# Feed-forward down products by Strassen's seven block products, placed between up products

## The chip, the cores and the metric

One core of a Trainium2 chip runs the whole program. The metric is the device time of one execution in microseconds (us), the median of several runs.

## What is computed

Two post-norm residual layers on 256 tokens of width 2048, all in float32. Layer 0 mixes tokens with a bidirectional gated linear attention, layer 1 with a two-dimensional neighbourhood attention. After each comes a gated feed-forward part, which the change is about:

```
D_FF = 11 * D_MODEL // 4                 # 5632, or 44 blocks of 128

def _conv_ffn(x, w_up, conv_w, conv_b, w_down):
    h = x @ w_up                         # 256 x 11264
    hp = jnp.pad(h, ((0, 0), (1, 1), (0, 0)))
    h = hp[:, :-2] * conv_w[0] + hp[:, 1:-1] * conv_w[1] + hp[:, 2:] * conv_w[2] + conv_b
    a, b = jnp.split(h, 2, axis=-1)
    return (jax.nn.gelu(a, approximate=False) * b) @ w_down

x = _layer_norm(DEEPNORM_ALPHA * x + f, ln_ffn_g[i], ln_ffn_b[i])
```

## The kernel before, in words

**Precision.** Every large product is made of three: each operand is split into a high part, which is the value rounded to the matrix unit's float32r type, and a low part, the rest. High times high, high times low and low times high are summed. `emit_split` (L129) does the split: a cast on ScalarE (L130), then a subtraction on VectorE (L131).

**Weights.** All weight matrices are cut into units of 1 MB, 128 x 2048 elements, and `unit_plan` (L48) lists them in the order of their use. SyncE's queue loads them (`emit_load`, L121) into three buffers, `pump` (L133) splits them in two halves, up to four units ahead of their use (NS = 4), with a scheduling rank 20 instructions later than where the split is written. `take` and `finish` (L159, L166) hand a unit to its product and release it. The framework orders each engine's instructions by rank and by its own estimate of when each is ready, and makes the semaphores; on the chip each engine then runs its list in order.

**Up products.** `ws_one` (L203) makes 128 channels of an up product for all 256 tokens: for each of 16 blocks of the width, a 512-column matmul (high part of the weights against high and low parts of both token halves) and a 256-column one (low part of the weights against the high parts). All matmuls go through `mm` (L191), so they share L192. The two halves of the sum stand in different columns of a PSUM bank, and `join` (L498) adds them: a copy on ScalarE, a sum on VectorE. `conv` (L673) does the middle tap on GpSimd (L684), and the outer taps on VectorE (L685, L686). `evac` (L692) applies GELU to the first of two channel blocks (L697), multiplies by the second (L702) and splits the product into gT, the operand of the down product. The first two channel blocks of each half come out of one wide product that is transposed ("pairs", `pair` at L714), with the middle tap on ScalarE (L682).

**Down products.** The 44 channel blocks are taken in three parts of 16, 16 and 12 (`THIRDS`, L39). After the up products of a part, `residual_out` (L367) runs its down product over four blocks of 512 columns: `as_block` (L218) takes the units (512 rows by 512 columns of the matrix), and makes 24 matmuls of 512 columns with each: 4 row blocks, 2 token halves, 3 parts. The result is added to the residual x_sb from PSUM (L381 for the first part, with the residual's factor, L383 for the others). After the last part the LayerNorm follows (`ln_mid`, L289, or `ln_last`, L328). In `ln_mid`, `turn` transposes the normalised rows and writes the next operand, and `resid` (L314) scales the residual and adds the bias with an accumulating DMA from GpSimd's queue (L318).

**PSUM.** Of eight banks five serve the products (`ps_mm`, L109), three the transposes and the attention (`ps_tp`).

**Attention.** `score` (L755) and `pv` (L790) each have bursts of six 256-column matmuls, in sums of three or six in PSUM.

Of the kernel before, what the change touches and what calls it, by code (L numbers as in the profile page):

```python
# [10 lines left out]
F32 = mybir.dt.float32  # L11
# [6 lines left out]
P = 128  # L18
# [17 lines left out]

FF = 11 * D // 4
NCT = FF // P
THIRDS = ((0, 16), (16, 16), (32, 12))  # L39

NS = 4
NR = 3
TP = 3
SPLIT_AFTER = 20
LN_BEFORE = 30


def unit_plan():  # L48

    plan = []  # L50
    for h in range(HG):
        plan += [("ws", "gla_in", h * 2 + c) for c in range(2)]
        plan += [("ws", "gla_in", 8 + h * 2 + c) for c in range(2)]
        if h == 0:
            plan += [("lr",)]
        plan += [("as", "gla_in", 4 + h, u) for u in range(4)]
        plan += [("as", "gla_in", 8 + h, u) for u in range(4)]
    plan += [("as", "gla_out", nb, u) for nb in range(4) for u in range(4)]
    for layer in range(DEPTH):
        if layer == 1:  # L60
# [5 lines left out]
        for c0, n in THIRDS:  # L66
            if c0 == 0:
                plan += [("pairs", f"up{layer}", u) for u in range(4)]
            for c in range(c0 + (2 if c0 == 0 else 0), c0 + n):
                plan += [("ws", f"up{layer}", c), ("ws", f"up{layer}", NCT + c)]  # L70
            plan += [("as", f"down{layer}", nb, u)
                     for nb in range(4) for u in range(c0 // 4, (c0 + n) // 4)]
    return plan


# [1 line left out]
def kernel(  # L77
# [16 lines left out]
    nc = tc.nc  # L94
    plan = unit_plan()
    n_units = len(plan)
    slot, n = {}, 0
    for j, u in enumerate(plan):
        slot[j] = n
        n += u[0] != "lr"  # L100
# [11 lines left out]
    def ps_tp():  # L112
        return psum.tile([P, 512], F32, tag="tp", name="ps_tp", bufs=TP)
# [4 lines left out]
    def pieces(n):  # L118
        return [slice(c * 2048 // n, (c + 1) * 2048 // n) for c in range(n)]

    def emit_load(j):  # L121
        r = raw_p.tile([P, 2048], F32, tag="raw", name="raw")
        if plan[j][0] == "lr":
            nc.sync.dma_start(r[:, :512], w_lr)
        else:
            nc.sync.dma_start(r, w[slot[j]])
        raws[j] = r

    def emit_split(src, hi, lo):  # L129
# [3 lines left out]
    def pump():  # L133
        while st["split"] < min(n_units, st["done"] + NS):
            j = st["split"]
            while st["load"] < min(n_units, j + NR):
                emit_load(st["load"])
                st["load"] += 1
            r = raws.pop(j)
# [51 lines left out]
    def mm(o, l, r, start, stop):  # L191
        nc.tensor.matmul(o, l, r, start=start, stop=stop)  # L192


    def ws_part(xs, hi, lo, ps, kcs):
        hi3 = hi.rearrange("p (k m) -> p k m", m=P)
        lo3 = lo.rearrange("p (k m) -> p k m", m=P)
        ps4 = ps.rearrange("p (t h n) -> p t h n", t=2, h=2)
        for kc in kcs:
            mm(ps, hi3[:, kc], xs[:, kc].rearrange("p t h n -> p (t h n)"), kc == 0, False)  # L200
            mm(ps4[:, :, 0], lo3[:, kc], xs[:, kc, :, 0], False, kc == KC - 1)

    def ws_one(xs, evac):  # L203
        hi, lo = take()
# [84 lines left out]
    def ln_mid(pool, xs, t, stats, idx, gb):  # L289

        def head():
            mv, rstd = ln_head(pool, xs, t, stats)
            for b in range(4):
                blk = xs[:, t, b * 512:b * 512 + 512]
                nc.vector.tensor_scalar(blk, blk, mv[:, 0:1], rstd, ALU.subtract, ALU.mult)  # L295

        def turn(b):
# [62 lines left out]
        return g  # L360

    def load_gb(pool, idx):
        b = pool.tile([P, D], F32, tag="b", name="b")
        nc.gpsimd.dma_start(b, lnp[idx, 1:2, :].broadcast_to([P, D]))
        return load_g(scope["xp"], idx), b

# [298 lines left out]
    def ffn(layer):  # L665
# [4 lines left out]
        cb = pool.tile([P, 2 * NCT], F32, name="cb")  # L670
        nc.gpsimd.dma_start(cb, convb[:, layer])

        def conv(i, ch, ps, joined=False):  # L673
            if joined:
                hh = ps
            else:
                hh = pool.tile([P, T], F32, tag="h", name="h", bufs=3)
# [3 lines left out]
            if joined:  # L681
                nc.scalar.activation(c, hh, AF.Identity, bias=cb[:, ch:ch + 1], scale=w_[:, 1:2])  # L682
            else:
# [5 lines left out]
        for part, (c0, n) in enumerate(THIRDS):  # L689
            held = {}  # L690

            def evac(i, ps, joined=False):  # L692
                kc = i // 2
                if i % 2 == 0:
                    c = conv(0, c0 + kc, ps, joined)
                    ge = pool.tile([P, T], F32, tag="ge", name="ge", bufs=2)
                    nc.scalar.activation(ge, c, AF.Gelu)  # L697
                    held["a"] = ge
                else:
                    c = conv(1, NCT + c0 + kc, ps, joined)  # L700
                    gg = pool.tile([P, T], F32, tag="gg", name="gg", bufs=2)
                    nc.vector.tensor_tensor(gg, held["a"], c, ALU.mult)  # L702
                    emit_split(gg.rearrange("p (t n) -> p t n", t=2), gT[:, kc, :, 0], gT[:, kc, :, 1])

            start = 0
            if part == 0:

                ht = {}

                def h_out(t, ps):  # L710
                    ht[t] = pool.tile([P, 512], F32, tag="ht", name="ht", bufs=2)
                    nc.scalar.copy(ht[t], ps)

                def pair(i):  # L714
                    tp = ps_tp()
                    for j in range(2):
                        for t in range(2):
                            nc.tensor.transpose(tp[:, j * T + t * P:j * T + t * P + P],
                                                ht[t][:, (2 * j + i) * P:(2 * j + i) * P + P], ident)
                    for j in range(2):  # L720
                        evac(2 * i + j, tp[:, j * T:j * T + T], True)

                as_block(xT, 4, h_out, apart=True, settle=True)
                later(lambda: pair(0), 1)
                later(lambda: pair(1), 1)
                start = 4
            for i in range(start, 2 * n):
                ws_one(xT, lambda ps: evac(i, ps))
            if part == 0:
                scope["gb"] = load_gb(pool, idx) if idx == 2 * DEPTH - 1 else load_g(scope["xp"], idx)  # L730
            residual_out(gT, part == 0, part == len(THIRDS) - 1, n // 4, idx)


    def attention():
# [110 lines left out]
def lay_out(a):  # L845
# [7 lines left out]
    plan = [u for u in plan if u[0] != "lr"]  # L853
    w = np.empty((len(plan), P, 2048), np.float32)
    for dst, unit in zip(w, plan):
        m = mats[unit[1]]
        if unit[0] == "pairs":
            u = unit[2]
# [56 lines left out]
```

## Time and profile before

| | |
|---|---|
| median of 3 runs | 2282.26 us (2282.12 to 2282.65) |
| the profiled execution's own time | 2282.44 us |
| its span, from the first to the last instruction | 2280.6 us |
| mean granted clock of the matrix unit | 0.998 of full speed |
| busy share of the span: TensorE, VectorE, ScalarE, GpSimd | 99%, 66%, 46%, 14% |
| moved by DMA | 439.02 MB |

The profile is of one execution. PE is the matrix unit's matmuls, PEld its weight loads, which run beside the matmuls; DVE is VectorE, ACT ScalarE, POOL GpSimd, SP SyncE. The ends of matmuls are modelled, so their starts are what counts; some records of matmuls can be missing. An instruction is named by its line, its engine, and what it writes and reads.

### The profile page before, as it was taken

The numbers are of one execution on the slowest core, as the hardware profiler recorded it, in microseconds if no ns is written. First come the engines' busy times: TensorE is split into PE (matmuls) and PEld (weight loads), VectorE is DVE, ScalarE is ACT, GpSimd is POOL, SyncE is SP. The second block draws the span as 40 slices with busy tenths as digits, with TensorE's granted clock in tenths as the row PEclk, the third lists the DMA queues.
The fourth block names the chain that finished last, engine by engine and source line by source line (L and its number), as shares of the span: only waits on it lengthen the run. The fifth ranks groups of instructions, "written<-read, shape, count | busy, mean of one in ns | idle before, by whom it ended". The sixth has DMA issues, their size and how long they took to land. (4 is left out here: it accounts for less than half of the span.)

```text
span 2280.6 us, 29636 instructions
## 1 busy us (share of the span) xinstructions
PE 2262.1 (99%) x11740; PEld 1925.1 (84%) x11740; DVE 1506.3 (66%) x2096; ACT 1056.7 (46%) x1537; POOL 317.7 (14%) x272
## 2 busy tenths in 40 slices
PE   9999999999999999999999999999999999999997
PEld 7888888888888888888888888888888888888886
DVE  7656656866656665676686666667676567756775
ACT  6654544544434444344464555446444444434442
POOL 1101000222002220122010100001220022201211
PEclk9999999999999999999999999999999999999999
DMA  8544464745554445555585555547446555565452
GB/s 279 187 168 169 182 243 157 250 184 185 203 188 181 185 178 209 186 184 185 185 258 187 194 189 198 202 165 240 176 176 227 195 175 179 183 216 188 174 198 93
DMA packets 66602, 439.02 MB, mean 193 GB/s; under 512 B 7648, under 2 KB 9952, under 8 KB 15136
## 3 DMA queue, kind: packets, MB, share of 16 engines
q1 hardware_dynamic: 60336, 415.00, 50.1%
q0 software_dynamic: 5840, 21.61, 3.8%
q8 instruction: 92, 1.51, 0.3%
q10 hardware_dynamic: 288, 0.52, 0.1%
q14 instruction: 46, 0.38, 0.0%
HBM read 431.87 MB, written 2.10 MB: 190 GB/s over the span
## 5 line engine op out<-in xcount | busy, mean ns | idle before, releaser
L131 DVE TENSOR_TENSOR lo<-raw,hi 128x1024 fp32r<-128x1024 f32 (+1 forms) x791 | 943.2, 1210 | 486.6 <-ACT hi L130 485.6
L192 PE MATMUL ps_mm<-xT,hi 128*128 128x512 f32 x3472 | 1229.3, 399 | 2.4 <-ACT hi L130 1.8
L130 ACT CAST hi<-raw 128x1024 fp32r<-128x1024 f32 (+1 forms) x791 | 806.7, 1041 | 514.3 <-PE ps_mm L192 485.1
L192 PE MATMUL ps_mm<-xT,lo 128*128 128x256 f32 x3472 | 974.5, 281 | 0.2 <-DVE lo L131 0.2
L192 PEld LDWEIGHTS ps_mm<-xT,hi 128*128 128x128 f32 x3472 | 651.7, 188 | 162.6 <-ACT hi L130 2.6
L192 PEld LDWEIGHTS ps_mm<-xT,lo 128*128 128x128 f32 x3472 | 655.3, 189 | 1.5 <-DVE lo L131 0.8
L192 PE MATMUL ps_mm<-hi,gT 128*128 128x512 f32 x1920 | 594.6, 390 | 0.0
L192 PEld LDWEIGHTS ps_mm<-hi,gT 128*128 128x128 f32 x1920 | 360.2, 188 | 74.5
L684 POOL TENSOR_SCALAR c<-h,cw,cb 128x256 f32<-128x256 f32 x168 | 239.0, 1422 | 1070.2 <-DVE h L503 1070.2
L192 PE MATMUL ps_mm<-lo,gT 128*128 128x512 f32 x960 | 373.5, 389 | 0.0
L192 PE MATMUL ps_mm<-hi,xT 128*128 128x512 f32 x896 | 284.1, 391 | 0.4 <-DVE xT L131 0.4
L192 PEld LDWEIGHTS ps_mm<-lo,gT 128*128 128x128 f32 x960 | 180.2, 188 | 37.2
L192 PEld LDWEIGHTS ps_mm<-hi,xT 128*128 128x128 f32 x896 | 167.9, 188 | 35.6 <-DVE xT L131 1.2
L192 PE MATMUL ps_mm<-lo,xT 128*128 128x512 f32 x448 | 174.8, 390 | 0.0
L130 ACT CAST gT<-gg 128x256 fp32r<-128x256 f32 x88 | 35.6, 407 | 285.4 <-DVE gg L702 285.4
L697 ACT ACTIVATE ge<-c 128x256 f32<-128x256 f32 x88 | 36.7, 417 | 251.4 <-DVE c L686 251.3
L685 DVE SCALAR_TENSOR_TENSOR c<-h,cw,c 128x255 f32<-128x255 f32 x168 | 81.3, 484 | 76.3 <-POOL c L684 76.3
L192 PEld LDWEIGHTS ps_mm<-lo,xT 128*128 128x128 f32 x448 | 84.2, 188 | 17.4 <-DVE rs_m L276 0.7
L686 DVE SCALAR_TENSOR_TENSOR c<-h,cw,c 128x255 f32<-128x255 f32 x168 | 81.3, 484 | 5.9
L502 ACT COPY join_t<-ps_mm 128x256 f32<-128x256 f32 x216 | 78.3, 363 | 1.8 <-issue 1.0
L503 DVE TENSOR_TENSOR h<-ps_mm,join_t 128x256 f32<-128x256 f32 x168 | 70.2, 418 | 5.2 <-ACT join_t L502 5.2
L131 DVE TENSOR_TENSOR gT<-gg,gT 128x256 fp32r<-128x256 f32 x88 | 37.7, 430 | 38.8 <-ACT gT L130 38.8
(139 smaller groups left out, 784.2 us busy)
## 6 DMA issues: line engine op xcount, KB each, us to landing
raw<-in_w_dram SPq DMA_DIRECT2D x388, 1024.0 KB, 4.8
x_sb<-in_lnp_dram POOLq DMA_DIRECT2D x6, 1024.0 KB, 10.6
g<-in_lnp_dram POOLq DMA_DIRECT2D x4, 1024.0 KB, 15.9
raw<-in_w_dram SPq DMA_DIRECT2D x12, 256.0 KB, 6.9
bt<-in_bias_dram POOLq DMA_DIRECT2D x16, 192.0 KB, 2.9
bt<-bmask_sb POOLq DMA_DIRECT2D x16, 192.0 KB, 3.1
xr<-in_xt_dram SPq DMA_DIRECT2D x8, 256.0 KB, 5.7
x_sb<-in_x_dram POOLq DMA_DIRECT2D x1, 2048.0 KB, 9.6
```

Source lines behind the costliest of these rows:

```text
L130: nc.scalar.copy(hi, src)
L131: nc.vector.tensor_tensor(lo, src, hi.bitcast(F32), ALU.subtract)
L192: nc.tensor.matmul(o, l, r, start=start, stop=stop)
L502: nc.scalar.copy(tmp, ps4[:, :, 1])
L503: nc.vector.tensor_tensor(dst.rearrange("p (t n) -> p t n", t=2), ps4[:, :, 0], tmp, ALU.add)
L684: nc.gpsimd.tensor_scalar(c, hh, w_[:, 1:2], cb[:, ch:ch + 1], ALU.mult, ALU.add)
L685: nc.vector.scalar_tensor_tensor(c[:, 1:], hh[:, :T - 1], w_[:, 0:1], c[:, 1:], ALU.mult, ALU.add)
L686: nc.vector.scalar_tensor_tensor(c[:, :T - 1], hh[:, 1:], w_[:, 2:3], c[:, :T - 1], ALU.mult, ALU.add)
L697: nc.scalar.activation(ge, c, AF.Gelu)
```

## The change

The first 32 of the 44 channel blocks now go through seven products for eight. They are cut into four portions of 8 blocks. With tokens in two halves, a portion's channels in two groups of four blocks, and the output in two pairs of column blocks, each pair is a 2 x 2 by 2 x 2 block product. The seven products are named q3, p1, q7, p2, q6, q5 and q4. The last 12 blocks go through `residual_out` as before.

- `operands` makes sums and differences of a portion's gated channels and splits them into gT (in place of what `evac` split).
- The weight operand of each product is a sum of blocks, made by DMA: a tile "x" receives block (1,1), then has the blocks (1,0), (0,0) and (0,1) (with the signs in the other operands) added by accumulating DMAs, each after the split that read the tile before. A tile "z" does the same with (0,0) and (1,0). p2 is a plain load on SyncE's queue. x and z are on GpSimd's queue.
- `seven` makes a product of 12 matmuls, accumulating some in one bank (p1, q6, q5 in one; q7, q4 in another), and `into` adds the bank to the residual blocks.
- A product stands between any two up units of the next portion, after the first two.
- Up units use `ws_half`: three 256-column matmuls per block of the width, summed in the same 256 columns of PSUM; `join` goes, and the middle tap is on ScalarE for all.
- Around this, `turn` uses one tile for four blocks, under the tag "x"; `resid` has earlier due times; the last gain and bias are loaded after the up products; the unit's places in memory are by key.

The diff, cut to its core:

```diff
-THIRDS = ((0, 16), (16, 16), (32, 12))
+PN = 8
+PORTIONS = 4
+LAST = 12
+SEVEN = ("q3", "p1", "q7", "p2", "q6", "q5", "q4")
+OF_X = {"q3": (1, 1), "q7": (1, 0), "q6": (0, 0), "q4": (0, 1)}
+OF_Z = {"p1": (0, 0), "q5": (1, 0)}
...
+        for p in range(PORTIONS):
+            ws = up_units(up, PN * (p + 1), PN)
+            seven = [("v", down, j, p, kind) for j in range(2) for kind in SEVEN]
+            plan += ws[:2]
+            for v, u in zip(seven, ws[2:]):
+                plan += [v, u]
...
+    def emit_chain(c):
+        j = chains[c].pop(0)
+        u = plan[j]
+        kind = u[4]
+        src = w[v_key(u, (OF_X if c == "x" else OF_Z)[kind])]
+        if kind in ("q3", "p1"):
+            held[c] = scope["pool"].tile([P, 2048], F32, tag=c, name=c)
+            nc.gpsimd.dma_start(held[c], src)
+        else:
+            nc.gpsimd.dma_start(held[c], src, accum_op=ALU.add)
...
             splits[j] = (hi, lo)
+            if chain and chains[chain] and plan[chains[chain][0]][1] == plan[j][1]:
+                emit_chain(chain)
...
+    def ws_half(xs, evac):
+        hi, lo = take()
+        ps = ps_mm()[:, :T]
...
+        for kc in range(KC):
+            mm(ps, hi3[:, kc], xs[:, kc, :, 0], kc == 0, False)
+            mm(ps, hi3[:, kc], xs[:, kc, :, 1], False, False)
+            mm(ps, lo3[:, kc], xs[:, kc, :, 0], False, kc == KC - 1)
+            if kc % 4 == 3:
+                tick()
+        evac(ps)
+        finish()
...
-            f = pool.tile([P, 4, P], F32, tag="ln_f", name="ln_f", bufs=2)
+            if b == 0:
+                cell["f"] = pool.tile([P, 4, 4, P], F32, tag="x", name="ln_f")
+            f = cell["f"][:, b]
...
-            slow.append((st["tick"] + 36 + 8 * b, lambda b=b: resid(b)))
+            slow.append((st["tick"] + 24 + 5 * b, lambda b=b: resid(b)))
...
-                join(pool, hh, ps)
...
-                nc.gpsimd.tensor_scalar(c, hh, w_[:, 1:2], cb[:, ch:ch + 1], ALU.mult, ALU.add)
+            nc.scalar.activation(c, hh, AF.Identity, bias=cb[:, ch:ch + 1], scale=w_[:, 1:2])
...
+        ops = {k: gT[:, 2 * i:2 * i + 2].rearrange("p k t h n -> p (k t) h n") for i, k in enumerate(SEVEN)}
+        def operands():
+            a11, a21 = sums[:, 0:4, 0], sums[:, 0:4, 1]
+            a12, a22 = sums[:, 4:8, 0], sums[:, 4:8, 1]
+            def part(kind, src):
+                emit_split(src, ops[kind][:, :, 0], ops[kind][:, :, 1])
+            part("p1", a11)
+            part("p2", a12)
+            nc.vector.tensor_tensor(a11, a21, a11, ALU.subtract)
+            part("q7", a11)
+            nc.vector.tensor_tensor(a11, a11, a22, ALU.subtract)
+            part("q6", a11)
+            nc.vector.tensor_tensor(a12, a11, a12, ALU.add)
+            part("q3", a12)
+            nc.vector.tensor_tensor(a21, a22, a21, ALU.subtract)
+            part("q5", a21)
+            neg = ops["q4"]
+            nc.scalar.mul(neg[:, :, 0], a22, -1.0)
+            nc.vector.scalar_tensor_tensor(neg[:, :, 1], a22, -1.0, neg[:, :, 0].bitcast(F32), ALU.mult, ALU.subtract)
...
+        def into(t, nb, ps, first, sub):
...
+            nc.vector.scalar_tensor_tensor(blk, blk, ALPHA if first else 1.0, ps, ALU.mult,
+                                           ALU.subtract if sub else ALU.add)
+        def seven(j, p, kind):
+            hi, lo = take()
...
+            bank = {"p1": "a", "q6": "a", "q5": "a", "q7": "c", "q4": "c", "p2": "p", "q3": "d"}[kind]
...
+            for kc in range(4):
+                for n, (l, r) in enumerate(((0, hi3), (0, lo3), (1, hi3))):
+                    nc.tensor.matmul(ps, o[:, kc, l], r[:, kc], start=new and kc == 0 and n == 0,
+                                     stop=kc == 3 and n == 2, skip_group_check=not new)
...
+        for p in range(PORTIONS):
+            operands()
+            todo = [(j, p, kind) for j in range(2) for kind in SEVEN]
+            for n, (ch, i) in enumerate((PN * (p + 1) + c, i) for c in range(PN) for i in range(2)):
+                if n >= 2:
+                    seven(*todo.pop(0))
+                up_one(i, ch)
...
-            residual_out(gT, part == 0, part == len(THIRDS) - 1, n // 4, idx)
+        residual_out(gT, False, True, LAST // 4, idx)
```

## Rows read from the trace of the kernel before

**Rows 1.** The page, busy us (share of the span) and instructions of each engine.
```profile
PE 2262.1 (99%) x11740; PEld 1925.1 (84%) x11740; DVE 1506.3 (66%) x2096; ACT 1056.7 (46%) x1537; POOL 317.7 (14%) x272
```

**Rows 2.** Stretches: length, busy us (instructions) by engine, granted clock, DMA share, GB/s.
```profile
440.00:1120.00 680.00, 680.00 (x3572) 581.10 (x3571) 445.86 (x599) 290.33 (x409) 116.53 (x82) 1.00 0.51 189
1557.00:2203.00 646.00, 646.00 (x3441) 553.26 (x3440) 426.69 (x586) 282.10 (x406) 116.20 (x82) 1.00 0.54 192
```

**Rows 3.** Timeline of PE in a down product: start us, us, instruction.
```profile
2203.19 0.39 PE L192 MATMUL ps_mm<-lo,gT 128*128 128x512 f32 x1
2203.42 0.61 PE L192 MATMUL ps_mm<-hi,gT 128*128 128x512 f32 x2
2203.87 0.39 PE L192 MATMUL ps_mm<-lo,gT 128*128 128x512 f32 x1
```

**Rows 4.** The chain that ended last, attention: start us, us, piece, matmuls.
```profile
1179.26 0.75 PE ps_tp L192 x6
1180.01 5.65 PE ps_mm L192 x32
...
1189.07 0.71 PE ps_tp L192 x6
...
1263.35 0.69 PE ps_tp L192 x6
```

**Rows 5.** Groups of instructions, shapes apart: count | busy us, mean ns | idle before.
```profile
L131 DVE TENSOR_TENSOR lo<-raw,hi 128x1024 fp32r<-128x1024 f32 x776 | 933.1, 1220 | 480.8 <-ACT hi L130 479.8 <-PE ps_mm L192 0.5
L130 ACT CAST hi<-raw 128x1024 fp32r<-128x1024 f32 x776 | 797.6, 1049 | 508.7 <-PE ps_mm L192 485.1 <-issue 9.9 <-DMA raw<-in_w_dram 8.4
...
L192 PEld LDWEIGHTS ps_mm<-xT,hi 128*128 128x128 f32 x3456 | 649.1, 188 | 161.5 <-ACT hi L130 2.6 <-DVE xT L131 1.1
...
L684 POOL TENSOR_SCALAR c<-h,cw,cb 128x256 f32<-128x256 f32 x168 | 239.0, 1422 | 1070.2 <-DVE h L503 1070.2
...
L685 DVE SCALAR_TENSOR_TENSOR c<-h,cw,c 128x255 f32<-128x255 f32 x168 | 81.3, 484 | 76.3 <-POOL c L684 76.3
...
L702 DVE TENSOR_TENSOR gg<-ge,c 128x256 f32<-128x256 f32 x88 | 37.4, 425 | 3.1
L697 ACT ACTIVATE ge<-c 128x256 f32<-128x256 f32 x88 | 36.7, 417 | 251.4 <-DVE c L686 251.3
...
L383 DVE TENSOR_TENSOR x_sb<-ps_mm,x_sb 128x512 f32<-128x512 f32 x32 | 21.8, 690 | 28.2 <-PE ps_mm L192 28.2
...
L131 DVE TENSOR_TENSOR xT<-ln_f,xT 128x512 fp32r<-128x512 f32 x24 | 15.8, 685 | 0.1
L130 ACT CAST xT<-ln_f 128x512 fp32r<-128x512 f32 x24 | 14.5, 621 | 3.9 <-DVE ln_f L311 3.8
...
L682 ACT ACTIVATE c<-ps_tp,cb,cw 128x256 f32<-128x256 f32 x8 | 4.5, 557 | 0.5 <-PE ps_tp L718 0.3
```

**Rows 6.** The stretch around the first LayerNorm; columns as in rows 2.
```profile
387.00:440.00 53.00, 52.45 (x272) 43.71 (x272) 49.98 (x82) 37.16 (x61) 7.25 (x6) 1.00 0.73 238
```

**Rows 7.** The page, DMA issues: count, KB each, us from issue to landing.
```profile
raw<-in_w_dram SPq DMA_DIRECT2D x388, 1024.0 KB, 4.8
```

**Rows 8.** Line 318, the accumulating DMAs of the LayerNorm bias: time to landing.
```profile
DMA to landing us min/median/max: 8.2/10.6/13.6
```

**Rows 9.** DMA queues and issues between 1542 and 1555 us.
```profile
q1 hardware_dynamic: 312, 2.29, 46.8%
q0 software_dynamic: 144, 1.05, 46.6%
...
x_sb<-in_lnp_dram POOLq DMA_DIRECT2D x1, 1024.0 KB, 8.4
```

More of the change, by code (lines that the diff above doesn't have):

```diff
@@ L45, with up_units, unit_keys @@
 LN_BEFORE = 30
+def up_units(up, c0, n):
+    n = min(n, NCT - c0) if c0 else n
+    if c0 == 2:
+        n = PN - 2
+    return [("ws", up, c + i) for c in range(c0, c0 + n) for i in (0, NCT)]
+def unit_keys(plan):
+    keys = {}
+    for u in plan:
+        if u[0] == "lr":
+            continue
+        if u[0] == "v":
+            _, m, j, p, kind = u
+            for nb, k in ((2 * j + 1, 2 * p + 1), (2 * j, 2 * p), (2 * j + 1, 2 * p), (2 * j, 2 * p + 1)):
+                keys.setdefault(("as", m, nb, k), len(keys))
+        else:
+            keys.setdefault(u, len(keys))
+    return keys
 def unit_plan():
@@ L65, in unit_plan @@
             plan += [("as", "na_out", nb, u) for nb in range(4) for u in range(4)]
[L66 to L72, printed above, removed]
+        up, down = f"up{layer}", f"down{layer}"
+        plan += [("pairs", up, u) for u in range(4)]
+        plan += up_units(up, 2, PN)
+        for p in range(PORTIONS):
[4 more added lines that the diff above has]
+                plan += [v, u]
+        plan += up_units(up, PN * (PORTIONS + 1), NCT - PN * (PORTIONS + 1))
+        plan += [("as", down, nb, u) for nb in range(4) for u in range(2 * PORTIONS, 2 * PORTIONS + LAST // 4)]
     return plan
@@ L96, with v_key @@
     n_units = len(plan)
[L97 to L100, printed above, removed]
+    keys = unit_keys(plan)
+    def v_key(u, cell):
+        _, m, j, p, _ = u
+        return keys[("as", m, 2 * j + cell[0], 2 * p + cell[1])]
     const = ctx.enter_context(tc.tile_pool(name="const", bufs=1))
@@ L119, in pieces @@
         return [slice(c * 2048 // n, (c + 1) * 2048 // n) for c in range(n)]
+    chains = {"x": [j for j, u in enumerate(plan) if u[0] == "v" and u[4] in OF_X],
+              "z": [j for j, u in enumerate(plan) if u[0] == "v" and u[4] in OF_Z]}
+    held = {}
+    def emit_chain(c):
[6 more added lines that the diff above has]
+            nc.gpsimd.dma_start(held[c], src)
+        else:
+            nc.gpsimd.dma_start(held[c], src, accum_op=ALU.add)
     def emit_load(j):
+        u = plan[j]
+        if u[0] == "v" and u[4] != "p2":
+            return
         r = raw_p.tile([P, 2048], F32, tag="raw", name="raw")
-        if plan[j][0] == "lr":
+        if u[0] == "lr":
             nc.sync.dma_start(r[:, :512], w_lr)
         else:
-            nc.sync.dma_start(r, w[slot[j]])
+            nc.sync.dma_start(r, w[v_key(u, (0, 1)) if u[0] == "v" else keys[u]])
         raws[j] = r
@@ L138, in pump @@
                 st["load"] += 1
-            r = raws.pop(j)
+            chain = None
+            if plan[j][0] == "v" and plan[j][4] != "p2":
+                chain = "x" if plan[j][4] in OF_X else "z"
+            r = held[chain] if chain else raws.pop(j)
             hi = hi_p.tile([P, 2048], F32R, tag="hi", name="hi")
@@ L362, in load_gb @@
     def load_gb(pool, idx):
-        b = pool.tile([P, D], F32, tag="b", name="b")
+        b = pool.tile([P, D], F32, tag="x", name="b")
         nc.gpsimd.dma_start(b, lnp[idx, 1:2, :].broadcast_to([P, D]))
@@ L687, in conv @@
             return c
[L689 to L730, printed above, removed]
-            residual_out(gT, part == 0, part == len(THIRDS) - 1, n // 4, idx)
@@ new lines, in ffn, with evac @@
+        gate = {}
+        def evac(i, ch, ps):
+            c = conv(i, i * NCT + ch, ps)
+            if i == 0:
+                nc.scalar.activation(c, c, AF.Gelu)
+                gate["a"] = c
+            else:
+                gg = sums[:, ch % PN]
+                nc.vector.tensor_tensor(gg.rearrange("p t n -> p (t n)"), gate["a"], c, ALU.mult)
+                if ch >= PN * (PORTIONS + 1):
+                    k = ch - PN * PORTIONS
+                    emit_split(gg, gT[:, k, :, 0], gT[:, k, :, 1])
@@ new lines, in up_one, with h_out, pair @@
+        def up_one(i, ch):
+            ws_half(xT, lambda ps: evac(i, ch, ps))
+        ht = {}
+        def h_out(t, ps):
+            if t == 0:
+                ht["all"] = pool.tile([P, 2048], F32, tag="z", name="ht")
+            ht[t] = ht["all"][:, t * 512:t * 512 + 512]
+            nc.scalar.copy(ht[t], ps)
+        def pair(i):
+            tp = ps_tp()
+            for j in range(2):
+                for t in range(2):
+                    nc.tensor.transpose(tp[:, j * T + t * P:j * T + t * P + P],
+                                        ht[t][:, (2 * j + i) * P:(2 * j + i) * P + P], ident)
+            for j in range(2):
+                evac(j, i, tp[:, j * T:j * T + T])
@@ new lines, in ffn @@
+        as_block(xT, 4, h_out, apart=True, settle=True)
+        later(lambda: pair(0), 1)
+        later(lambda: pair(1), 1)
+        for ch in range(2, PN):
+            if ch == 5:
+                emit_chain("x")
+                emit_chain("z")
+            for i in range(2):
+                up_one(i, ch)
+        scope["gb"] = load_g(scope["xp"], idx) if idx < 2 * DEPTH - 1 else None
+        ops = {k: gT[:, 2 * i:2 * i + 2].rearrange("p k t h n -> p (k t) h n") for i, k in enumerate(SEVEN)}
@@ new lines, in ffn @@
+        for p in range(PORTIONS):
[4 more added lines that the diff above has]
+                    seven(*todo.pop(0))
+                up_one(i, ch)
+        for k in range(PN):
+            emit_split(sums[:, k], gT[:, k, :, 0], gT[:, k, :, 1])
+        for ch in range(PN * (PORTIONS + 1), NCT):
+            for i in range(2):
+                up_one(i, ch)
@@ L734, in attention @@
+        if idx == 2 * DEPTH - 1:
+            scope["gb"] = load_gb(pool, idx)
+        residual_out(gT, False, True, LAST // 4, idx)
     def attention():
@@ L852, in lay_out @@
     plan = unit_plan()
-    plan = [u for u in plan if u[0] != "lr"]
-    w = np.empty((len(plan), P, 2048), np.float32)
-    for dst, unit in zip(w, plan):
+    keys = unit_keys(plan)
+    w = np.empty((len(keys), P, 2048), np.float32)
+    for unit, place in keys.items():
+        dst = w[place]
         m = mats[unit[1]]
```

41 lines of the change are left out of this document (33 added, 8 removed).

## The prediction

> **What bounds the kernel now.** The page's busy times come first: the matrix unit's matmuls fill 99% of the span, its weight loads 84%, VectorE 66%, ScalarE 46% [rows 1]. An average hides stages, so the stretches are next: in the two long stretches of up and down products TensorE is busy for every microsecond of 680 and of 646, at the full granted clock, while VectorE has about 66% [rows 2]. So TensorE waits for nothing there. The kernel gets faster only if TensorE gets less to stream, and stays faster only if VectorE, ScalarE and the DMA queues still deliver every operand in time.
>
> The unit prices of TensorE come from starts, since the ends are modelled. A 512-wide matmul in a down product follows the last by (2203.87 - 2203.19) / 3 = 0.227 us [rows 3]. An up unit of `ws_one` (16 pairs, 512 and 256 wide) takes 5.65 us [rows 4]. 256-wide matmuls in a row, three to a sum in PSUM, exist only in attention, in 32 bursts of six: 0.69 to 0.75 us, 24 of them 0.71, so 0.118 each [rows 4].
>
> **The products.** A portion is 8 row blocks of the down matrix. For one pair of 512-column blocks it was 4 units of 24 matmuls, 96; seven products of 12 are 84. With 2 pairs, 4 portions and 2 layers that is 16 x 12 = 192 matmuls fewer: 192 x 0.227 = **-43.6 us**. The first two channels, the last 12 and the attention lose no matmul.
>
> **The up units.** Per layer 84 units change from 32 matmuls (768 columns per block, as 512 + 256) to 48 of 256: the same columns, half as many weight loads again. 48 x 0.118 = 5.68 against 5.65 us: 168 x 0.03 = **+5 us**. The shortest burst gives 48 x 0.115 = 5.52 (-22 us), the longest 48 x 0.125 = 6.00 (+59 us). I take the common one, and keep both ends. The join (a ScalarE copy and a VectorE sum) goes, and so does GpSimd's 1.42 us per unit. VectorE waited 76.3 us in all for that step [rows 5], but TensorE didn't [rows 2]: 0.
>
> **What VectorE and ScalarE get, per portion.** TensorE needs 16 x 5.68 + 14 x 12 x 0.227 = 129 us. VectorE [rows 5]: 30 unit splits of 2 x 1.22 = 73.2; 16 convolutions of 2 x 0.484 = 15.5; 8 gate products of 0.425 = 3.4; 11 operand instructions of 0.685 = 7.5; 16 block updates from PSUM of 0.69 = 11.0. Together 110.6 us, 86% of 129. ScalarE: 30 x 2 x 1.05 + 16 x 0.557 + 8 x 0.417 + 7 x 0.62 = 79.6 us, 62%. Nearest row for whether that can be hidden: between 387 and 440 us VectorE is 94% and ScalarE 70% busy, and TensorE still works 52.45 of 53 us [rows 6]. Four units are split ahead of their use, which is the cover: 0. With the cover used up, the six more unit splits a portion would show with 6 x 2 x 1.22 = 14.6 us.
>
> **The burst between portions** is on the path. `operands` needs the last gate of the portion, and the first product (q3) comes after two more up units, 2 x 5.68 = 11.4 us. From the end of the last up unit: convolution 0.56 + 2 x 0.48, gate 0.43, 1.95 us. Then as written on VectorE: low parts of p1 and p2, a difference, q7's low part, a difference, q6's, a sum, q3's. That is 8 x 0.685 + 3 x (0.62 + 0.1) for the high parts that ScalarE makes in between, 7.6 us, and 0.5 for p2's: q3 stands at 10 us, just in time. But q5 and q4 follow ahead of the lower-ranked unit splits, 3 x 0.685 + 0.72 = 2.8, and the split of the third up unit takes 2.4: it stands at 15.3, and TensorE wants it at 11.4 + 2.7 = 14.1. So I put 1.2 us on each of 8 portions, **+10 us**. Lower end: the splits fit into VectorE's waits, 0. Upper end: at each of four ScalarE steps a unit split of 1.22 us goes first, 5 us a portion, +40. I take 1.2, since the order worked out gives it. Behind the waiting VectorE stands the next convolution, which frees a PSUM bank; of five banks two can be held by running sums, and three are left, so TensorE gets two units further before it waits for a bank.
>
> **The weight sums by DMA.** SyncE's queue loses 64 loads of 1 MB and gains 16 (p2). GpSimd's queue gains 96: 32 plain, 64 accumulating, each behind the split that last read its tile. Plain 1 MB loads of SyncE land in 4.8 us [rows 7]; the accumulating ones of the LayerNorm bias take 8.2 to 13.6 [rows 8], and 8.4 with only SyncE's loads beside them, where 1.05 MB held 46.6% of 13 us, 6.1 us of all DMA engines [rows 9]. A link of the x chain is landing, split (1.05 + 1.05 + 1.22, 4 us with its hops), next DMA. Per portion six accumulate at about 10 us and two are plain at about 7 (between SyncE's 4.8 and 8.4): 6 x 14 + 2 x 11 = 106 us of 129. The engines' load per portion: 8 x 6.1 + 22 x 2.7 (46.8% of 13 us for 2.29 MB [rows 9]) = 108 of 129, 84%; now it is 51 to 54% [rows 2]. Inside the cover: 0. Without cover each late link shows whole, up to 13.6 + 4 - 16.1 = 1.5 us on a link.
>
> Edits with one answer: the LayerNorm's wider tile, the earlier residual blocks, the shared tags x and z and the late load of the last gain and bias are work that was there before; the last load ends some 12 x 24 x 0.227 = 65 us before its reader: 0. What follows the last down product doesn't change: 0.
>
> **The sum.** The profiled execution took 2282.44 us (span 2280.6 and 1.8 around it), against a median of 2282.26, so they are one time. 2282.4 - 43.6 + 5 + 10 = **2254 us**.
>
> **Rivals.** (1) *VectorE eats the gain.* The burst costs 4 to 5 us a portion and its backlog, at 86% load, up to 2 more: 32 to 56 us over 8 portions, 2276 to 2300 us. For: VectorE stood 480.8 us waiting in front of the low parts [rows 5], and such waits are lost when it is the bound. Against: the 94% stretch [rows 6]. 0.15.
>
> (2) *The x chain sets the pace: slower.* Place: the accumulating DMA between two splits. Eight links share 129 us, so it decides from 16.1 us a link. If all take the 13.6 us of the longest landing [rows 8], a link is 17.6 and a portion 141: +12 x 8 = 96, and the burst hides in it: 2282 - 39 + 96 = 2339 us. For: two chains on one queue, and DMA engines at 84%. Against: 8.4 us beside SyncE's loads [rows 9], and plain loads at two links of eight. 0.09.
>
> (3) *Weight loads become the bound: slower.* A load reads 188 ns [rows 5], and 2688 - 192 = 2496 are added. If none overlapped the next, an up unit would be 48 x 0.188 = 9.0 us and the kernel 168 x 3.4 = 570 us longer. The bursts fit six loads and six matmuls into 0.71 us [rows 4], so loads do overlap; but six are no stream of 48. It decides from 5.65 + 34 / 168 = 5.85 us a unit, 0.122 a load; at the longest burst's 0.125 the kernel takes 2282 - 44 + 59 + 10 = 2307 us. 0.06.
> The Trainium skill, page "Perfetto Trace Analysis", section "Identifying the Most-Contended Engine", judges TensorE's headroom by the summed time of its weight loads over the window, not by that of its matmuls. By that rule 1925 + 2496 x 0.188 = 2394 us of loads would not fit into the span, an estimate of some 110 us slower; that loads of 0.188 us start 0.118 apart in the bursts speaks against it.
>
> (4) *It isn't what it says:* the compiled order leaves only one up unit ahead of q3. Then 5.7 us of cover are missing at q3, which waits 10 - 5.7 = 4.3, and the third unit 1.2 more: 8 x 5.5 = 44, 2288 us. 0.02.
>
> **How the numbers follow.** The forecast, with stalls of 0 to 4 us a portion and up units between 5.52 and 5.70, has 0.68 and a range of its own of 2232 to 2276 us. A difference under 0.2%, 4.6 us, a measurement of this kernel can't tell from none. Faster: 0.68, and 0.03 of rival 1. Same: 0.08 of rival 1. Slower: 0.04 of rival 1, 0.09, 0.06 and 0.02. The range takes the forecast and rivals 1 and 4, up to 2300; outside lie rivals 2 and 3 and a little at the fast end.
>
> **What would show it.** 14236 matmuls (11740 + 2688 - 192). Up units of 5.6 to 5.7 us in the chain; at 6.0 the second step is wrong. TensorE idle ahead of q3 and of the third up unit of each portion for 0 to 4 us; at more than 5 the burst is mis-sized. VectorE near 86% in the new stretches. Accumulating DMAs that land in 8 to 12 us, and ScalarE waiting for the tiles x and z under 20 us in all; if it waits there portion after portion, rival 2 holds. More than 60 us of idle TensorE in the up and down stretches would make the forecast wrong.

## The result, and the profile after

The changed kernel takes 2263.04 us (median of 4 runs, 2262.09 to 2263.6) against 2282.45 us of the kernel before in the same job: ratio 0.9915, 95% interval 0.9902 to 0.9927, 19.4 us less. The profiled execution took 2262.09 us, of which 2260.4 are the span. The forecast was 2254 us, with a range of 2232 to 2300.

The engines' busy times of the page after, in the form of [rows 1]:

```profile
PE 2240.8 (99%) x14236; PEld 2034.1 (90%) x14236; DVE 1600.3 (71%) x2144; ACT 1195.6 (53%) x1625; POOL 151.8 (7%) x200
```

The matmuls number 14236, as worked out. TensorE stays at 99%, so a gain can only be less to stream. The stretches of [rows 2], the first portion of layer 1's products by itself, and two stretches in the attention, with the same columns:

```profile
440.00:1120.00 680.00, 680.00 (x4822) 641.91 (x4822) 504.69 (x644) 365.91 (x461) 36.05 (x47) 1.00 0.75 230
1557.00:2203.00 646.00, 646.00 (x4706) 615.33 (x4705) 487.15 (x627) 360.76 (x460) 35.74 (x47) 1.00 0.77 237
```
```profile
1627.78:1757.90 130.12, 130.12 (x935) 123.25 (x934) 100.88 (x127) 73.43 (x91) 9.08 (x12) 1.00 0.82 243
```
```profile
1190.40:1192.00 1.60, 1.39 (x8) 1.22 (x9) 1.60 (x4) 1.18 (x3) 0.86 (x1) 0.88 0.00 0
1192.00:1196.00 4.00, 4.00 (x19) 3.47 (x18) 2.47 (x5) 2.27 (x4) 0.00 (x0) 0.62 0.98 283
```

In the product stretches TensorE is busy for every microsecond, at the full clock: none of the new waits reaches it. In a portion VectorE has 78% (100.88 of 130.12) and the DMA engines 82%. The last two rows are in the one stage that got worse, and come up below.

Where the time went is read from the first LayerNorm transpose of each stage, three before and three after (PE's timeline: start us, us, instruction):

```profile
387.29 0.27 PE L301 MATMUL ps_tp<-ident,x_sb 128*128 128x128 f32 x1
1131.91 0.27 PE L301 MATMUL ps_tp<-ident,x_sb 128*128 128x128 f32 x1
1519.56 0.38 PE L301 MATMUL ps_tp<-ident,x_sb 128*128 128x128 f32 x2
```
```profile
387.12 0.27 PE L375 MATMUL ps_tp<-ident,x_sb 128*128 128x128 f32 x1
1119.74 0.27 PE L375 MATMUL ps_tp<-ident,x_sb 128*128 128x128 f32 x1
1513.05 0.27 PE L375 MATMUL ps_tp<-ident,x_sb 128*128 128x128 f32 x1
```

The spans end at 2280.6 and 2260.4. So the feed-forward of layer 0 takes 732.6 us for 744.6 (-12.0), the attention of layer 1 takes 393.3 for 387.65 (**+5.7**, in a stage whose matmuls the change leaves alone), and the rest, layer 1's feed-forward with the tail, 747.3 for 761.1 (-13.7). With the 0.2 us ahead of the first of these starts, that sums to the -20.2 us between the two spans.

The chain that ended last, after (start us, us, piece, matmuls), in a portion:

```profile
1627.94 2.75 PE ps_mm L849 x12
1630.68 5.75 PE ps_mm L249 x48
1636.44 2.75 PE ps_mm L849 x12
```

Products and up units follow each other without a hole, 8.50 us a couple. A product costs 12 x 0.229 us, near the 0.227 of [rows 3]. The up unit costs 5.75 where [rows 4] had 5.65 and the forecast 5.68. 5.75 / 48 is 0.120 a matmul: over the 8,000 or so steps of this kind in the trace the median of the starts' distances is 120.0 ns for each of the three kinds of pair. Before, in the stretches of [rows 2], the 512-wide step had 236.4 on average and the 256-wide one 116.9: 353.3 ns a block, 5.653 us for the 16 blocks of a unit, where three of 120 make 360 and 5.76.

### The profile page after: what moved, and what is told of

Same layout as the page of the kernel before. It is cut to its first block, busy times and chain, and to the rows that moved or that the text cites. A ratio compares the mean times of both kernels' runs of the same rounds, so it can differ in the third digit from the quotient of the medians.

```text
span 2260.4 us, 34682 instructions
## 1 busy us (share of the span) xinstructions
PE 2240.8 (99%) x14236; PEld 2034.1 (90%) x14236; DVE 1600.3 (71%) x2144; ACT 1195.6 (53%) x1625; POOL 151.8 (7%) x200
## 3 DMA queue, kind: packets, MB, share of 16 engines
q1 hardware_dynamic: 53424, 364.67, 43.6%
## 5 line engine op out<-in xcount | busy, mean ns | idle before, releaser
L249 PE MATMUL ps_mm<-xT,hi 128*128 128x256 f32 (+1 forms) x6160 | 1252.8, 298 | 1.2 <-ACT hi L182 0.6
L183 DVE TENSOR_TENSOR lo<-raw,hi 128x1024 fp32r<-128x1024 f32 (+1 forms) x695 | 828.9, 1208 | 498.6 <-ACT hi L182 497.5
L182 ACT CAST hi<-raw 128x1024 fp32r<-128x1024 f32 (+1 forms) x695 | 708.3, 1038 | 757.9 <-PE ps_mm L249 550.6
L249 PEld LDWEIGHTS ps_mm<-xT,hi 128*128 128x128 f32 x6160 | 993.3, 191 | 45.4 <-ACT hi L182 1.8
L249 PEld LDWEIGHTS ps_mm<-hi,gT 128*128 128x128 f32 x896 | 168.2, 188 | 34.7
L849 PEld LDWEIGHTS ps_mm<-hi,gT 128*128 128x128 f32 x896 | 168.7, 188 | 33.0
L849 PE MATMUL ps_mm<-lo,gT 128*128 128x512 f32 x448 | 175.7, 392 | 0.0
L249 PE MATMUL ps_mm<-lo,gT 128*128 128x512 f32 x448 | 174.6, 390 | 0.0
L183 DVE TENSOR_TENSOR lo<-x,hi 128x1024 fp32r<-128x1024 f32 x128 | 151.5, 1218 | 5.6 <-ACT hi L182 5.1
L182 ACT CAST hi<-x 128x1024 fp32r<-128x1024 f32 x128 | 128.6, 1045 | 37.6 <-PE ps_mm L849 12.4
L754 ACT ACTIVATE c<-ps_mm,cb,cw 128x256 f32<-128x256 f32 x168 | 94.1, 560 | 0.0
L835 DVE SCALAR_TENSOR_TENSOR x_sb<-x_sb,ps_mm 128x512 f32<-128x512 f32 x128 | 85.9, 676 | 0.0
```

Source lines behind the costliest of these rows:

```text
L182: nc.scalar.copy(hi, src)
L183: nc.vector.tensor_tensor(lo, src, hi.bitcast(F32), ALU.subtract)
L835: nc.vector.scalar_tensor_tensor(blk, blk, ALPHA if first else 1.0, ps, ALU.mult, ALU.subtract if sub else ALU.add)
L849: nc.tensor.matmul(ps, o[:, kc, l], r[:, kc], start=new and kc == 0 and n == 0, stop=kc == 3 and n == 2, skip_group_check=not new)
```

## The experiments

Each time is a median; the ratio, with its 95% interval, is to the kernel before in the same job.

### The up units alone

The kernel before, with only the up units changed: three 256-wide matmuls a block, no join, the middle tap on ScalarE.

```diff
-                ws_one(xT, lambda ps: evac(i, ps))
+                ws_half(xT, lambda ps: evac(i, ps, True))
```

> The kernel before, with its 168 narrow up units made by `ws_half` (48 matmuls of 256 columns, summed in one place) and the middle tap on ScalarE; no Strassen. Theory (a 256-wide matmul in a stream starts 120.0 ns after the last, as in the changed kernel's trace): 168 x (48 x 0.120 - 5.65) = +18 us, 2300 us, TensorE without idle time. Rival, the prediction's step (118 ns, from the bursts of six): +5 us, 2287 us. Second rival, freed queues buy time (no join, no GpSimd step): 2282 us or less.

Measured: 2300.13 us, ratio 1.0077 (1.0062 to 1.0092), +18.0 us. The up units are a loss of 168 x (5.76 - 5.653) = 18 us by themselves, 8.9 us in each feed-forward part and nothing in the attention, and lifting the join from ScalarE and VectorE, and the tap from GpSimd, gives nothing back.

### Strassen with the old up units

The seven products kept, but up units as `ws_one` makes them, with the join.

```diff
-            ws_half(xT, lambda ps: evac(i, ch, ps))
+            def out(ps):
+                hh = pool.tile([P, T], F32, tag="h", name="h", bufs=1)
+                h3, ps4 = hh.rearrange("p (t n) -> p t n", t=2), ps.rearrange("p (t h n) -> p t h n", t=2, h=2)
+                nc.scalar.copy(h3, ps4[:, :, 1])
+                nc.vector.tensor_tensor(h3, ps4[:, :, 0], h3, ALU.add)
+                evac(i, ch, hh)
+            ws_one(xT, out)
```

> The changed kernel with the up units made as before (32 matmuls of 512 and 256 columns, halves joined by a ScalarE copy and a VectorE sum), products by seven for eight kept. Theory (TensorE is the bound in both, and a narrow unit costs 5.76 us against 5.65): 168 x 0.107 = 18 us less, 2245 us. Rival (the join is what VectorE had no room for: 0.42 us more per unit, some 92% of a portion, waits ahead of q3 with TensorE's clock halved after them): 2263 us or slower.

Measured: 2246.84 us, ratio 0.9845 (0.983 to 0.9859), 16.2 us faster than the changed kernel. Its chain and its stretches, in the same columns as above:

```profile
1630.11 5.64 PE ps_mm L249 x32
1635.75 2.74 PE ps_mm L855 x12
```
```profile
440.00:1120.00 680.00, 679.51 (x3574) 579.60 (x3573) 544.63 (x742) 405.59 (x559) 36.08 (x47) 1.00 0.75 231
1557.00:2203.00 646.00, 643.95 (x3405) 549.67 (x3404) 520.11 (x707) 391.30 (x539) 35.77 (x47) 1.00 0.77 236
```

Layer 0's feed-forward takes 723.2 us, 21.4 less than before: 96 x 0.227 = 21.8 was the forecast for the products alone. VectorE and ScalarE carry the join (VectorE has 742 instructions for 644 in the first stretch, ScalarE 559 for 461) and TensorE loses 2.5 us in 1326, most of it in one hole of 2 us ahead of a first product. The attention is still 4.6 us longer than in the kernel before. So the two halves of the change had opposite signs, and only one was needed.

### Less cover ahead of the first product

One up unit instead of two ahead of q3.

```diff
-            plan += ws[:2]
-            for v, u in zip(seven, ws[2:]):
+            plan += ws[:1]
+            for v, u in zip(seven, ws[1:]):
...
-                if n >= 2:
+                if n >= 1 and todo:
```

> The changed kernel with one up unit instead of two between a portion's last gate and its first product q3. Theory (in the changed kernel's trace q3's operand stands 8.75 us after the end of the last up unit, as the compiled order splits p1 ahead; cover falls from 11.5 to 5.76): 3.0 us of idle TensorE ahead of each q3, 8 x 3.0 = +24 us, 2287 us. Rival, the prediction's order (10 us to q3, the third unit's split 1.2 us later still): 5.5 us each, +44, 2307 us. Second rival (the order is rearranged again and hides it): 2263 us.

Measured: 2304.17 us, ratio 1.0096 (1.0081 to 1.0111), 41 us slower than the changed kernel. The same hole of 3.19 us (3.31 from start to start, less one step of 0.12) stands ahead of q3 in each of the 8 portions. PE's timeline at one, and the granted clock after it (columns as in [rows 2]):

```profile
1639.79 0.28 PE L250 MATMUL ps_mm<-xT,lo 128*128 128x256 f32 x1
1643.10 0.80 PE L850 MATMUL ps_mm<-hi,gT 128*128 128x512 f32 x1 [3.03 <-ACT gT L183]
```
```profile
1643.00:1646.00 3.00, 2.90 (x8) 2.47 (x9) 3.00 (x6) 1.13 (x3) 0.00 (x0) 0.50 0.87 180
1646.00:1650.00 4.00, 4.00 (x16) 3.28 (x15) 1.59 (x2) 1.04 (x2) 0.00 (x0) 0.62 0.47 152
1650.00:1654.00 4.00, 4.00 (x36) 4.00 (x35) 2.36 (x2) 1.24 (x2) 0.85 (x1) 1.00 0.26 111
```

So with one unit of 5.76 us, q3 stands 8.95 us after the portion's last up unit; the two units of the changed kernel, 11.52 us, would leave 2.6 us to spare, and its own trace shows 2.0 (below). The holes explain 8 x 3.19 = 25.5 of the 41 us. The rest, 2 us a portion on average, goes with the clock that follows: a granted clock of 0.50, which is 1.2 GHz, and a full one only some 7 us later. That is layer 1, where all four holes are followed by 6.8 us at 0.50 and a portion costs 2.8 us more than its hole. In layer 0 three of the four are followed by 3.4 us at 0.50, one by none (1.00 from 769.5 to 776 us), and a portion costs 1.3 us more than its hole. Rival 4 was right about the mechanism: what it described is what this kernel does, at 41 us where the prediction worked out 44 by other parts (4.3 of waiting and 1.2 of a late third unit, no clock).

### The x chain loaded twice

Each accumulating DMA of the x chain is issued twice, so the sums hold those blocks twice.

```diff
-            nc.gpsimd.dma_start(held[c], src, accum_op=ALU.add)
+            for _ in range(2 if c == "x" else 1):
+                nc.gpsimd.dma_start(held[c], src, accum_op=ALU.add)
```

> The changed kernel in which each accumulating DMA of the x chain is done twice (the weight sums hold those blocks twice). Theory (the chain has slack now, and is the pace once eight links need more than a portion's 130 us): six links of 8.1 + 8.1 + 0.6 + 4 = 20.8 and two of 10 are 145 us, 14 us over, 8 x 14 = +112, 2375 us. Rival (the chain is hidden well beyond that, since transfers overlap splits of other units): 2263 to 2270 us.

Measured: 2543.01 us, ratio 1.1141 (1.1121 to 1.1161), +280 us against the changed kernel, far over what was expected. The waits from 1557 us on (engine, line, what for: us in total, times, longest us), a stretch of layer 0 (as in [rows 2]) and the page's DMA issues:

```profile
ACT hi L183 <- DMA x<-in_w_dram: 289.3, 25, 16.0
POOL x L169 <- DMA x<-in_w_dram: 209.2, 24, 11.2
```
```profile
440.00:640.00 200.00, 179.84 (x1290) 169.15 (x1289) 119.92 (x157) 86.13 (x113) 13.76 (x17) 0.96 0.78 221
```
```profile
x<-in_w_dram POOLq DMA_DIRECT2D x112, 1024.0 KB, 9.5
z<-in_w_dram POOLq DMA_DIRECT2D x32, 1024.0 KB, 13.6
```

ScalarE now waits for x in nearly every link, TensorE is idle for a tenth of the stretch and its mean clock falls to 0.96. So rival 2's mechanism is real and its limit is near: one more accumulation of 8 to 9.5 us a link passes it. In the changed kernel it isn't reached. Beside x itself, the doubled DMAs hold up z on the same queue (13.6 us against 8.1), and the holes cost clock. How the 280 us divide among these was not separated.

### What the attention lost

After: TensorE stands idle for 4.16 us from the last matmul that starts ahead of it, at 1186.33 us (one step of 0.12 taken off), to 1190.61. Then comes the stretch at 0.62 of the clock that was shown above; within it the clock is 0.50 for 3.4 us, which costs some 1.7 us (an estimate: half of it). The two make up about the 5.7 us. The chain through it, and GpSimd's timeline:

```profile
1179.30 7.49 DMA bt<-bmask_sb
1186.89 0.77 DVE s L919 x2
1190.61 0.72 PE ps_tp L937 x4
1191.33 4.34 PE ps_mm L249 x16
```
```profile
1160.46 0.87 POOL L394 DMA_DIRECT2D x_sb<-in_lnp_dram  x1 [3.33 <-DVE x_sb L392]
1161.03 0.85 POOL L435 DMA_DIRECT2D g<-in_lnp_dram  x1
1168.76 0.55 POOL L896 DMA_DIRECT2D bt<-in_bias_dram  x1 [6.88 <-DVE s L919]
1179.30 0.88 POOL L897 DMA_DIRECT2D bt<-bmask_sb  x1 [9.99 <-DMA bt<-in_bias_dram]
```

The second head's bias (bt) stands on GpSimd's queue behind the LayerNorm's accumulating bias (x_sb) and the gain (g), takes 10 us to land where the median of the 16 takes 2.8, and the score, the softmax and the transposes of P wait for it. Two parts of the change could have moved it, the earlier due times of the residual blocks and the wide LayerNorm tile; a third kernel moves a load off the queue.

Due times as before for the attention's LayerNorm:

```diff
-            slow.append((st["tick"] + 24 + 5 * b, lambda b=b: resid(b)))
+            due = (36, 8) if idx == 1 else (24, 5)
+            slow.append((st["tick"] + due[0] + due[1] * b, lambda b=b: resid(b)))
```

> The changed kernel with the old due times (36 + 8 per block) for the residual of the one LayerNorm ahead of the attention. Theory (the earlier residual puts its accumulating DMA and the next gain's load ahead of the second head's bias in GpSimd's queue, and the scores wait for it): the 4.2 us that TensorE stands idle in the attention go, and up to 5.7 us of the stage, 2257 to 2259 us. Rival (the attention lost its time to something else, such as the state of the queues after the weight sums): 2263 us, the idle time stays.

Measured: 2263.43 us, ratio 0.9916 (0.9901 to 0.9931): no difference. GpSimd's order is the same and the hole is 5.2 us. My theory fell.

The gain of that stage loaded from SyncE's queue instead:

```diff
-        nc.gpsimd.dma_start(
+        (nc.sync if idx == 2 else nc.gpsimd).dma_start(
```

> The changed kernel with the load of the attention's LayerNorm gain (1 MB, not needed for another 350 us) on SyncE's queue in place of GpSimd's. Theory (in GpSimd's queue this load and the accumulating one stand ahead of the second head's bias, which takes 10 us to land and then 7.5 to be masked): the bias lands some 5 us earlier, the idle 4.2 us and the half clock after it go, 2257 to 2259 us. Rival (the accumulating DMA alone delays it, or SyncE's weights are delayed as much): 2263 us.

Measured: 2258.5 us (2256.36 to 2260.21), ratio 0.9895 (0.988 to 0.991); the hole shrinks to 2.5 us. What stands ahead on the queue matters. How much of it the gain is, stays open: the hole of 2.5 us is that of a run of 2260.21 us, and the shortest run, 2256.36, is as short as those of the next kernel, which has no hole.

Small LayerNorm tiles, two tags in turn, in place of one wide tile under "x":

```diff
-            if b == 0:
-                cell["f"] = pool.tile([P, 4, 4, P], F32, tag="x", name="ln_f")
-            f = cell["f"][:, b]
+            f = pool.tile([P, 4, P], F32, tag="xz"[b % 2], name="ln_f")
```

> The changed kernel with `turn`'s tile back to one block each (tags x and z in turn) in place of one tile for four blocks. Theory (the wide tile changed the order in which VectorE gets the LayerNorm's work, which made the residual's DMA 5.7 us later ahead of the attention, and the second head's scores late): the idle 4.2 us at the attention's second head go, 2257 to 2259 us. Rival (the lateness comes from the queue's loads alone): 2263 us, the idle time stays.

Measured: 2256.9 us (2256.33 to 2257.24), ratio 0.9888 (0.9871 to 0.9904), 6.1 us faster than the changed kernel. The hole is gone and the attention takes 387.7 us, as before. GpSimd's timeline:

```profile
1155.20 1.17 POOL L392 DMA_DIRECT2D x_sb<-in_lnp_dram  x1
1155.76 1.15 POOL L433 DMA_DIRECT2D g<-in_lnp_dram  x1
1169.42 0.55 POOL L894 DMA_DIRECT2D bt<-in_bias_dram  x1 [12.51 <-DVE s L917]
1175.83 0.88 POOL L895 DMA_DIRECT2D bt<-bmask_sb  x1 [5.86 <-DMA bt<-in_bias_dram]
```

The accumulating x_sb is issued 14.2 us ahead of the head's bias, not 8.3 (before it was 14.2 too, 1166.87 and 1181.10), and the bias takes 4 us less to land. With the wide tile the compiled order held the residual work back. By which dependence it did so wasn't traced.

### Grouping the widths

The kernel before, with four 512-wide matmuls and then four 256-wide ones, not in turn.

```diff
         for kc in kcs:
             mm(ps, hi3[:, kc], xs[:, kc].rearrange("p t h n -> p (t h n)"), kc == 0, False)
+        for kc in kcs:
             mm(ps4[:, :, 0], lo3[:, kc], xs[:, kc, :, 0], False, kc == KC - 1)
```

> The kernel before with another order of the matmuls in `ws_part`: of four blocks of the width first the four 512-wide ones, then the four 256-wide ones, in place of pairs. Nothing else. Theory (a 512-wide step is 0.2267 and a 256-wide one 0.120 among their own kind, 0.3467 together, and a pair in turn takes 0.3537; the 7 ns belong to the change of width): 16 x 7 ns x 3/4 = 0.086 us a unit, 217 units, -18 us, 2264 us. Rival (the 7 ns belong to the 256-wide matmul's divided output columns or to its operand, wherever it stands): 2282 us.

Measured: 2276.14 us, ratio 0.9973 (0.9963 to 0.9984), -6 us. PE's timeline:

```profile
1799.77 1.09 PE L192 MATMUL ps_mm<-xT,hi 128*128 128x512 f32 x4
1800.70 0.63 PE L192 MATMUL ps_mm<-xT,lo 128*128 128x256 f32 x4
1801.17 1.09 PE L192 MATMUL ps_mm<-xT,hi 128*128 128x512 f32 x4
```

Four of each kind take 1.40 us against 4 x 0.3533 = 1.413. The theory's 18 us did not come. The change of width is the smaller part of what makes the 512-wide step 236.4 ns: among themselves these matmuls still have 234 (median of the starts' distances), where a down product's have 227. What the rest comes from is open.

### The parts together

Old up units and small LayerNorm tiles; then the grouping as well, all three edits being those above.

> The seven products kept, up units with the wide matmul and the join as in the kernel before, and the LayerNorm's transposed rows in small tiles of their own. My theory: the two losses are independent, so the times add up: 2246.8 us of the wide up units, less the attention stage's 4 to 6 us, is 2241 to 2243 us, with the attention stage back at 387 to 388 us and no idle matrix unit in it. Rival: the order that the framework compiles shifts with each edit, and the idle time turns up elsewhere (ahead of a portion's first product, where 2 us were seen): 2247 us or more.

> The kernel of the run with wide up units and small LayerNorm tiles, with each block of four widths' four 512-wide matmuls first and its four 256-wide ones after. In the kernel before this grouping alone gave 6.1 us over its 376 or so units of this kind. My theory: the same per unit, so 5 to 6 us below the run without it, 2235 to 2238 us. Rival: the gain of the grouping belonged to another place than the up units' stream (a wait that moved): then no difference, 2241 to 2243 us.

Measured: 2237.66 us (2236.0 to 2238.7), ratio 0.9803 (0.9788 to 0.9818), and 2233.75 us (2232.86 to 2234.92), ratio 0.9788 (0.9772 to 0.9805). The first is 3 us better than the sum, 2240.7, and below the 2241 to 2243 expected: the attention is at 387.8 us, and the 2 us hole ahead of a first product that the wide up units alone had is gone too. The second takes off another 3.9 us in the medians, less than the 5 to 6 expected (5.7 between the two profiled spans). The chain of the second:

```profile
1628.45 5.59 PE ps_mm L249 x32
1634.04 2.77 PE ps_mm L854 x12
```

The up unit falls from 5.64 to 5.59 us (168 x 0.05 = 8 us), but each of 112 products costs 0.02 us more (2 us): in this trace the step from one high part of the weights to the next (ps_mm<-hi,gT) has a median of 236 ns, where the first of the two kernels has 227. Why is open. This is the best version: 48.7 us faster than the kernel before, 29.3 than the changed one.

## Why the prediction was right, and where its terms were not

**The products: right.** -43.6 us for 192 matmuls. With the old up units layer 0's feed-forward gave 21.4 of its 21.8 us.

**The up units: the step that was mis-sized.** Forecast +5 us, measured +18.0 alone. "256-wide matmuls in a row ... 0.118 each" was the wrong price for this stream, by 1.7 ns, on 168 x 48 = 8064 matmuls: 5.76 us a unit and not 5.68, 13 us in all. More digits would not have helped: the steps of the 32 bursts have a median of 118 ns (188 of them from 113 to 124, and four of 157 to 160, which are the pieces of 0.75). The bursts of the attention are cheaper than the stream of 48, and it is the price of the form itself, in a long run, that was missing. The bounds, 0.115 to 0.125, did hold it. What makes the difference is open.

**The burst: forecast +10, measured 0.** The order as written on paper put all of `operands` after the last gate (L769) and the third up unit's split after that. VectorE and ScalarE on the chip, in the middle of a portion and at its end:

```profile
1584.15 0.69 DVE L183 TENSOR_TENSOR gT<-sums,gT 128x512 fp32r<-128x512 f32 x1 [0.69 <-ACT gT L182]
1584.88 0.69 DVE L817 TENSOR_TENSOR sums<-sums 128x512 f32<-128x512 f32 x1
1588.55 0.68 DVE L183 TENSOR_TENSOR gT<-sums,gT 128x512 fp32r<-128x512 f32 x1
...
1617.41 1.23 DVE L183 TENSOR_TENSOR lo<-raw,hi 128x1024 fp32r<-128x1024 f32 x1 [2.61 <-ACT hi L182]
1618.95 1.21 DVE L183 TENSOR_TENSOR lo<-raw,hi 128x1024 fp32r<-128x1024 f32 x1
...
1620.59 0.42 DVE L769 TENSOR_TENSOR sums<-c 128x256 f32<-128x256 f32 x1
1621.05 0.69 DVE L819 TENSOR_TENSOR sums<-sums 128x512 f32<-128x512 f32 x1
1621.58 0.63 ACT L826 ACTIVATE gT<-sums 128x512 fp32r<-128x512 f32 x1
1621.66 0.68 DVE L823 TENSOR_TENSOR sums<-sums 128x512 f32<-128x512 f32 x1
1622.26 1.28 DVE L183 TENSOR_TENSOR gT<-sums,gT 128x512 fp32r<-128x512 f32 x2
...
1625.27 0.68 DVE L183 TENSOR_TENSOR gT<-sums,gT 128x512 fp32r<-128x512 f32 x1
```

Three of the eleven VectorE instructions (p1's low part, the difference L817, q7's low part) need the first four blocks only and ran 32 us or more ahead of the last gate. Of the other eight, two of the three block sums (L819, L823) run ahead of the low parts, so VectorE waits for none of the ScalarE steps. The last low part, q3's, ends at 1625.95 us, 4.9 us after the last gate and 2 us before q3's piece starts at 1627.94. The third up unit's split (L183, 1617.41 and 1618.95) ran ahead of the gate, so it could not be late, and TensorE has no hole in the stretch. But it held the gate back: the gate ended at 1621.01, 4.6 us after the last up unit's end (1627.94 less two units of 5.76), not 1.95. So q3 stood after 9.5 us, close to the 10 of the forecast, by two errors that cancelled: a later gate and a shorter burst. The cover is thin: with one unit less every portion had a hole.

**VectorE: 86% forecast, 78% measured.** The count was right, 60 + 32 + 8 + 11 + 16 = 127, which is the row's x127. The 9.7 us too many are mostly in the durations: neighbours overlap in the record (L755 from 1618.56 for 0.47, the next from 1618.95), so that the durations of the 127 add up to 109.5 us where the busy time is 100.88. Rival 1 falls: with the old up units VectorE carries even the join, at 80% of both stretches, and TensorE loses 2.5 us there, not 32 to 56.

**The DMA chains: right at 0.** The 64 accumulating DMAs land in 7.9 to 12.1 us, median 8.6 (8 to 12 forecast), and ScalarE's waits for x and z by the groups of the profile after:

```profile
L182 ACT CAST hi<-x 128x1024 fp32r<-128x1024 f32 x128 | 128.6, 1045 | 37.6 <-PE ps_mm L849 12.4 <-DMA x<-in_w_dram 8.6 <-PE ps_mm L249 6.1
```

8.6 us in all, under the 20 promised. Rival 2 did not happen; the doubled chain shows that its limit is near.

**Weight loads: not over rival 3's limit.** It decided from 0.122 us a load; the matmuls, with a load to each, start 0.120 apart. Whether the load or the matmul sets the 0.120, no run separates. The loads read 191 ns each, so 14236 x 0.19 = 2.7 ms of them lie in a span of 2.26 ms in which TensorE is busy for 99%: loads overlap in a long stream as they did in bursts of six. The Trainium skill, page "Perfetto Trace Analysis", section "Identifying the Most-Contended Engine", has TensorE's headroom judged by MFU (the FLOPs done against the peak) and by the loads' summed time over the window. For the second measure this trace doesn't agree: the sum is 120% of the window. The prediction's use of the rule added 2496 durations to 1925 us of busy time, in which overlapping loads count once; that busy time grew by 109 us, to 2034.

**Edits with one answer: not 0.** "The LayerNorm's wider tile, the earlier residual blocks ... are work that was there before: 0" missed +5.7 us in the attention. The due times were indeed worth nothing; the wide tile wasn't. Here the changed buffer changed the compiled order, and with it the place of a load in GpSimd's queue.

**The sum.** -43.6 + 18 + 0 + 5.7 = -19.9, against -20.2 between the spans. The forecast missed by 9 us because +13 and +5.7 that it lacked met 10 that it had too many; that the errors partly cancelled is luck. The sign and the range were right for the reason given, the products; the other three terms of the sum were not.

## What to carry to other kernels

Where TensorE never waits, take apart a change into what it takes off TensorE's stream and what it puts on, and price each by the median start-to-start of that very form in a long run, not by a short burst of another one: here a second edit that came along and took the join away cost 18 of 44 us, and the engines it relieved had room. Before a cover is counted, ask of each instruction of the burst what it needs, and not where the source has it: some may run long before, and others may go ahead of them. And an edit of a tile's shape or tag is an edit of the schedule; look for it in stages that the change wasn't about.

## What was not expected of the hardware

- A 256-wide matmul in a stream costs 120.0 ns, where half of a 512-wide one of the down products costs 113.5 (227). The Trainium skill, page "TensorE: Matmul & The Clock Gate", section "Back-to-back issue gap", gives N / 2.4 + 2.5 ns for isolated matmuls of N columns, 109.2 and 215.8 ns by estimate, and 131 ns for N = 512 in a stream with weight loads. This trace, a float32r stream with a weight load to each matmul, agrees with neither: it has 13 to 14 ns above N / 2.4 at either width.
- In the kernel before, 512-wide matmuls with the tokens moving take 236 ns a step (median), those of the down products 227, and grouping the widths takes the first to 234 only. The cause is open.
- A hole of 3.2 us in TensorE's work was followed, in seven of eight cases, by a granted clock of 0.50, for 3.4 us in layer 0 and 6.8 us in layer 1, and cost 1.3 and 2.8 us more than itself on average.
- An accumulating DMA of 1 MB on GpSimd's queue lands in 8.6 us (median of 64), a plain one of SyncE's queue in 4.9, and one more in each accumulating link of the x chain took ScalarE's waits for x from 8.6 us in the whole run to 289 us from 1557 us on, and the time up by 280 us.
